# Mixer A's tiles first with the projections spread over them, mixer B's by blocks of tokens with the output projection beside them

## The chip, the cores and the metric

The kernel runs on one core of a Trainium2 chip. The metric is the device time of one execution in microseconds. The engines named here are PE (TensorE: matmuls and transposes; PEld is its weight load), DVE (VectorE), ACT (ScalarE), POOL (GpSimd) and SP (SyncE, which issues the DMAs). Each takes its instructions in the order of its own queue.

## What is computed

One step of a one-layer encoder over 1024 prompt rows and 32 sample rows, 1024 wide, all in float32: a SwiGLU layer, a sub-layer of two attention mixers, and a second SwiGLU layer. The change lies in the middle one.

```python
h = adaln_in(x, gains[2], sh2, sc2)
qa, ka, va, qb, kb, vb = jnp.split(h @ w_in, SPLITS, axis=-1)
# mixer A: 8 heads x 64; a row reads its own chunk of 64 and the 8 before, clipped relative bias
# mixer B: 8 query heads, 2 key/value heads; own chunk and the 2 before, bucketed bias, sinks
oa, ob, rows = mixers(qa, ka, va, qb, kb, vb)
o = jnp.concatenate([rmsnorm(oa, group_gains[:WIDTH_A]),
                     rmsnorm(ob, group_gains[WIDTH_A:])], axis=-1) @ w_out
x = x + g2[:, None] * rmsnorm(o, gains[3])
```

The newest key and value rows of both mixers are outputs too.

## The kernel before

The 1056 rows are kept in three blocks of 384, 384 and 288 columns (`TB`), features on the partitions. [...]

**Projections.** `qk_proj` (L670) makes one query or key unit, two heads wide: for each block 24 matmuls into the bank `pq`. `v_proj` (L653) makes a value unit, 256 columns wide: for each of nine tiles of rows 24 matmuls into `pv`. There are four query and four key units for A (`load_qa`, `load_ka`), two value units for A (`load_va`), four query units for B (`load_qb`), and one unit with the keys and values of B. Before the tiles start, a loop over the blocks (L1069) runs B's key/value unit, B's query unit 0 and A's value unit 0, each block as soon as its normalised input `h2` is there (`need`). That input comes from `between` (L496): the residual with its norm, then the next norm. In both norms the squares are folded on DVE and POOL, PE sums them over the partitions (`pss`), DVE takes nine small steps for the reciprocal root (`ry`), and PE broadcasts it (`pr`).

**Tiles.** An attention tile is a pair of heads `p` and 128 rows `i`. `TileB` (L780) has two matmul pairs for the scores (`Sb`), an addition of the bias and a maximum on DVE, exponentials on ACT, a scaling, transposes on PE (`ppb`), and the product with the values (`po`). `TileA` (L718) is the same with up to 640 keys (`S`, `pp`, `po`). `TileS` (L847) is the sample's tile of a pair (`Ss`, `pps`). The list `tiles` (L1094) has 72 of them: B's four pairs (36 tiles), A's pairs 0 and 1 (18), then A's pairs 2 and 3 interleaved (18). The loop at L1232 walks over the list. A tile's scores are issued two tiles ahead for B and one for A (`lead`).

**What goes beside the tiles.** `fill` issues pieces of the remaining projections at an even rate, in two stages (`STAGES`, by tile number): over tiles 0 to 34 the units of B's queries 1 to 3, A's values 1 and A's K and Q of pair 0, over 37 to 54 the K and Q of pairs 1 to 3. `group_norm(tb, g)` normalises a block of B's output (g = 1) or A's (g = 0). It needs all four pairs of that mixer in the block. `out_piece` makes one eighth of the output projection of a block (24 matmuls, bank `wo`). It needs both group norms of the block. Five pieces are issued within the tile loop (`OUTS`), 19 after it.

**The order.** The order in which the source issues work is only a priority: a scheduler at build time moves instructions within each engine's queue, and pools of buffers bound how far (eight slots in `wpool` for weights, keys, queries and values; five in `hpool`; two double banks for scores).

Of the kernel before, what the change touches and what calls it, by code (L numbers as in the profile page):

```python
# [21 lines left out]
DEC = 32  # L22
# [18 lines left out]
GN1 = 55  # L41
# [16 lines left out]
PRIME = 0  # L58
PFILL = 5
KEARLY = 1  # L60
# [6 lines left out]
STAGES = ((0, 34), (37, 54))  # L67
RATE = 1.0
OUTS = (0,) * 13 + (1,) * 5
LAG = 0.5  # L70
# [4 lines left out]
def encoder_step(ctx: ExitStack, tc, x_prompt, x_sample, cache_a_k, cache_a_v, cache_b_k, cache_b_v,  # L75
# [66 lines left out]
    jp = consts.tile([128, 128], I32, name="jp")  # L142
# [637 lines left out]
    class TileB:  # L780
# [14 lines left out]
        def qk(self, hh):  # L795
            if hh:
                return
            p, i, k0, nt = self.p, self.i, self.k0, self.nt
            c, L = p // 2, 128 * nt
            T = self.T  # L800
            bias = prep[("B", p)]["bias"]
            S = p2("Sb")
            for h in range(2):
                cols = slice(128 * k0, 128 * k0 + L)
                te.matmul(S[:, h, :L], T[:, h, :], KSB[:, c, cols], start=True, stop=False)
                te.matmul(S[:, h, :L], T[:, 2 + h, :], KSB[:, c, cols], start=False, stop=True)
            ve.tensor_tensor(S[:, :, :L], S[:, :, :L], bias[:, :, 256 - L:256], op=OP.add)
            nm = small.tile([128, 2], F32, name="nmb")
            ve.tensor_reduce(nm, S[:, :, :L], axis=AX.X, op=OP.max, negate=True)
# [29 lines left out]
        def av(self):  # L839
# [4 lines left out]
               lambda j, h, kn: kvb[:, k0 + j, 128 + 64 * c:192 + 64 * c],  # L844
               O[tb][:, 4 + p, 128 * cc:128 * cc + 128])

    class TileS:  # L847
# [53 lines left out]
        def av(self):  # L901
# [6 lines left out]
            else:  # L908
                c = p // 2

                def vsl(j, h, kn):
                    return (cbv if j == 0 else kvbs[:, 128:256])[:kn, 64 * c:64 * c + 64]
# [10 lines left out]
    def start_qb(p, w):  # L923
# [3 lines left out]
        qs = small.tile([128, DEC], F32, name="qbs", bufs=2)  # L927
# [40 lines left out]
    def flow_ka(p, w):  # L968
# [3 lines left out]
        piece = qk_proj(w, KQ[:, 0, :], KQs[:, 0, :], 1.0)  # L972
# [3 lines left out]
    def flow_qa(p, w):  # L976
        KQ, KQs = kqa[p]
        piece = qk_proj(w, KQ[:, 1, :], KQs[:, 1, :], 0.125)
        for tb in range(3):
            yield from piece(tb)  # L980
# [43 lines left out]
    wkv, wq0, wv0 = split_vcols(w_in, 2048), load_qb(0), load_va(0)  # L1024
    kvb = wpool.tile([128, 8, 256], F32, name="vt", tag="w")
    kvbs = small.tile([32, 256], F32, name="vs", bufs=3)
    kv_piece, q0_piece, v0_piece = v_proj(wkv, kvb, kvbs), start_qb(0, wq0), start_va(0, wv0)
# [17 lines left out]
    def keys_new(t0, n):  # L1045

        pk = KBANK("pk", (128, 4, 128))
        for j in range(n):
            te.transpose(pk[:, j, :], kvb[:, t0 + j, 0:128], ident)
        for c in range(2):  # L1050
            cols = slice(128 * t0, 128 * (t0 + n))
            pkc = pk[64 * c:64 * c + 64, 0:n].rearrange("p a b -> p (a b)")
            ae.activation(KSB[0:64, c, cols], pkc, AF.Copy)
            ve.tensor_tensor(KSB[64:128, c, cols], pkc, KSB[0:64, c, cols], op=OP.subtract)

    def keys_sample():
        pk = KBANK("pk")
        te.transpose(pk[:, :DEC], kvbs[:, 0:128], ident[:DEC, :DEC])
# [4 lines left out]
    def rows_b():  # L1063
        dma.dma_start(nbk_p[0, 0].rearrange("t h d -> t (h d)"), kvb[:, 7, 0:128])
        dma.dma_start(nbv_p[0, 0].rearrange("t h d -> t (h d)"), kvb[:, 7, 128:256])
        dma.dma_start(nbk_s[0, 0].rearrange("t h d -> t (h d)"), kvbs[:, 0:128])
        dma.dma_start(nbv_s[0, 0].rearrange("t h d -> t (h d)"), kvbs[:, 128:256])

    for tb in range(3):  # L1069
        need(("h2", tb))  # L1070
        if tb == 0:
            keys_cached()
        for x in token_tiles(tb):
            run(kv_piece(*x))
        if tb == 2:
            KSB = wpool.tile([128, 2, 1024], F32R, name="KSB", tag="w")
            if PRIME:
                primed.append(load_qb(1))
            keys = [lambda: keys_new(0, 4), lambda: keys_new(4, 4), keys_sample]
        if tb == 2 and KEARLY == 1:  # L1080
            keys.pop(0)()
        run(q0_piece(tb))
        for i, x in enumerate(token_tiles(tb)):
            run(v0_piece(*x))
            if tb == 2 and KEARLY:
                keys and keys.pop(0)()
    for k in keys:
        k()
    rows_va(0)
    rows_b()  # L1090
# [4 lines left out]
    for kind, p in [("B", p) for p in range(4)] + [("A", 0), ("A", 1)]:  # L1095
        opens[len(tiles)] = [(kind, p)]
        tiles.append(TileS(kind, p))
        tiles += [(TileB if kind == "B" else TileA)(p, i) for i in range(8)]
    for _, p, i in sorted((i + LAG * (p - 2) + (0 if i < 0 else 0), p, i) for p in (2, 3) for i in range(-1, 8)):
        if i < 0:  # L1100
            opens[len(tiles)] = [("A", p)]
        tiles.append(TileA(p, i) if i >= 0 else TileS("A", p))
    whole = [max(n for n, t in enumerate(tiles) if isinstance(t, TileA) and t.i // 3 == tb) for tb in range(3)]
# [22 lines left out]
    COST = {"B": 10.6, "V": 23.4, "K": 10.6, "A": 10.6}  # L1126
# [78 lines left out]
    def lead(t):  # L1205

        return LEAD_B if t < 36 else 1

    ready.add(("B", 0))
# [15 lines left out]
    with tc.manual_schedule(engines={mybir.EngineType.PE}) if MANUAL else ExitStack():  # L1225
# [3 lines left out]
        if PRIME == 2:  # L1229
            now = flow(flows[0][2])  # L1230
            fill(PFILL)
        for n in range(N):  # L1232
            for first, last, units in flows:
                if n == first:
                    now = now if PRIME == 2 and n == 0 else flow(units)
                    rate = sum(COST[key[0]] for key, _, _ in units) / (last - first) / 2 * RATE
# [6 lines left out]
            for _ in range(OUTS[n - 54] if n >= 54 else 0):  # L1243
# [14 lines left out]
            for _, last, _ in flows:  # L1258
                if n == last - 1:
                    fill(1e6)  # L1260
                    budget = 0.0
    tiles[N - 1].av()
    begin(("gn", 2, 0), group_norm(2, 0), first=True)
# [84 lines left out]
```

## Time and profile before

| | |
|---|---|
| three runs | 2225.36, 2229.99, 2230.26 us; median 2229.99 |
| profiled execution | 2232.07 us, its span 2230.3 us |
| granted TensorE clock, mean | 0.983 |
| mixer sub-layer within the span | 847 us (first `pv`) to 1429 us (last `wo`) |
| first score of B / of A | 933.0 us / 1084.9 us |

The span is the time from the first to the last instruction of the program, and the rest of an execution lies around it. In a row of a timeline the number in brackets is how long the engine stood idle before the instruction, and what ended that. In a row of groups the idle time stands behind the second bar. The rows of the profile stand in the prediction, where they are used.

### The profile page before, as it was taken

Reading aid. Unit: us, or ns where it says so; the run is one execution under the profiler, and the core shown is the slowest. Engines: PE = TensorE matmul, PEld = TensorE weight load, DVE = VectorE, ACT = ScalarE, POOL = GpSimd, SP = SyncE. Lnnn points to the kernel's source line nnn. Section 1 sums busy time; section 2 is a strip of 40 time slices with the busy share of each in tenths; the row PEclk is TensorE's granted clock in tenths of the full one; section 3 lists DMA queues with packets and bytes.
Section 4 is the critical chain, followed back from the end, with each engine's and each line's share of the span. In section 5 each row is a group of like instructions: output and inputs, shape, how many; then the busy total and the mean of one; then the engine's idle time right before and its main releaser. Section 6 shows DMA issues by size and latency. Waiting matters only on the chain.

```text
span 2230.3 us, 33962 instructions
## 1 busy us (share of the span) xinstructions
PE 2163.1 (97%) x14012; PEld 2069.8 (93%) x14012; DVE 1238.6 (56%) x2425; ACT 698.1 (31%) x1450; POOL 180.5 (8%) x281
## 2 busy tenths in 40 slices
PE   6989999999999999899999899999999999999998
PEld 4989999999999999899788579999999999999998
DVE  5735677765643497677544775775433333333336
ACT  4411111111111253566544763433111111111133
POOL 2100000000000022100110413320000000000000
PEclk8999999999999999899999899999999999999999
DMA  9245344343321353110211221523211111111122
GB/s 328 85 76 125 105 122 132 104 123 95 104 76 57 90 162 121 59 31 20 68 30 30 77 59 56 161 81 104 85 57 39 44 43 47 57 38 55 41 67 81
DMA packets 200350, 186.00 MB, mean 83 GB/s; under 512 B 7340, under 2 KB 169540, under 8 KB 199044
## 3 DMA queue, kind: packets, MB, share of 16 engines
q1 hardware_dynamic: 200196, 183.84, 27.7%
q8 instruction: 110, 1.80, 0.3%
q14 instruction: 44, 0.36, 0.1%
HBM read 160.98 MB, written 22.84 MB: 82 GB/s over the span
## 4 chain that ended last, share of the span: by engine, by line
PE 84%; DMA 7%; DVE 6%; ACT 1%; issue 1%; POOL 1%; SPq 0%; DVEq 0%; ACTq 0%; POOLq 0%
PE dn L316 7%; PE up L316 7%; PE up L318 7%; PE up L317 7%; PE dn L317 7%; PE dn L318 7%; PE gate L318 7%; PE gate L317 7%; PE gate L316 7%; DMA raw<-in_w_up_dram 4%; PE po L705 3%; PE S L744 2%; PE pq L316 2%; PE pq L318 2%; PE pq L317 2%; PE pp L768 1%
## 5 line engine op out<-in xcount | busy, mean ns | idle before, releaser
L316 PE MATMUL up<-h_hi,w 128*128 128x384 f32 (+1 forms) x1056 | 341.1, 323 | 9.2 <-ACT sl L541 9.2
L316 PE MATMUL dn<-gg,w 128*128 128x384 f32 (+1 forms) x1056 | 340.8, 324 | 3.9 <-DVE facc L572 3.5
L317 PE MATMUL gate<-h_lo,w 128*128 128x384 f32 (+1 forms) x1056 | 340.1, 322 | 3.9 <-DVE h_lo L437 3.9
L316 PE MATMUL gate<-h_hi,w 128*128 128x384 f32 (+1 forms) x1056 | 341.2, 323 | 0.0
L317 PE MATMUL up<-h_lo,w 128*128 128x384 f32 (+1 forms) x1056 | 340.8, 323 | 0.0
L317 PE MATMUL dn<-gg,w 128*128 128x384 f32 (+1 forms) x1056 | 339.8, 322 | 0.6 <-DVE gg L545 0.6
L318 PE MATMUL up<-h_hi,w 128*128 128x384 f32 (+1 forms) x1056 | 340.4, 322 | 0.0
L318 PE MATMUL gate<-h_hi,w 128*128 128x384 f32 (+1 forms) x1056 | 340.4, 322 | 0.0
L318 PE MATMUL dn<-gg,w 128*128 128x384 f32 (+1 forms) x1056 | 339.4, 321 | 0.0
L572 DVE TENSOR_TENSOR facc<-dn,facc 128x768 f32<-128x768 f32 (+1 forms) x240 | 212.7, 888 | 221.4 <-PE dn L318 221.3
L295 DVE TENSOR_TENSOR w<-raw,w 128x1024 fp32r<-128x1024 f32 x187 | 232.3, 1250 | 170.7 <-ACT w L294 163.6
L294 ACT ACTIVATE w<-raw 128x1024 fp32r<-128x1024 f32 x187 | 195.8, 1056 | 278.0 <-PE dn L318 103.5
L541 ACT ACTIVATE sl<-gate 128x384 f32<-128x384 f32 (+1 forms) x132 | 60.9, 462 | 549.6 <-PE gate L318 549.5
L542 DVE TENSOR_TENSOR sl<-sl,up 128x384 f32<-128x384 f32 (+1 forms) x132 | 68.5, 519 | 282.3 <-PE up L318 282.0
L316 PEld LDWEIGHTS up<-h_hi,w 128*128 128x128 f32 x1056 | 199.1, 189 | 9.5 <-ACT sl L541 9.5
L316 PEld LDWEIGHTS dn<-gg,w 128*128 128x128 f32 x1056 | 198.7, 189 | 5.8 <-DVE facc L572 4.8
L317 PEld LDWEIGHTS gate<-h_lo,w 128*128 128x128 f32 x1056 | 198.7, 188 | 4.5 <-DVE h_lo L437 4.5
L317 PEld LDWEIGHTS dn<-gg,w 128*128 128x128 f32 x1056 | 198.7, 188 | 1.2 <-DVE gg L545 1.2
L318 PEld LDWEIGHTS up<-h_hi,w 128*128 128x128 f32 x1056 | 199.4, 189 | 0.0
L317 PEld LDWEIGHTS up<-h_lo,w 128*128 128x128 f32 x1056 | 199.2, 189 | 0.0
L316 PEld LDWEIGHTS gate<-h_hi,w 128*128 128x128 f32 x1056 | 198.9, 188 | 0.1
L318 PEld LDWEIGHTS gate<-h_hi,w 128*128 128x128 f32 x1056 | 198.7, 188 | 0.0
(224 smaller groups left out, 3365.3 us busy)
## 6 DMA issues: line engine op xcount, KB each, us to landing
raw<-in_w_mod_dram SPq DMA_DIRECT2D x56, 512.0 KB, 4.0
raw<-in_w_gate_dram SPq DMA_DIRECT2D x54, 512.0 KB, 3.9
raw<-in_w_up_dram SPq DMA_DIRECT2D x54, 512.0 KB, 4.6
raw<-in_w_down_dram SPq DMA_DIRECT2D x54, 512.0 KB, 4.5
raw<-in_w_in_dram SPq DMA_DIRECT2D x18, 512.0 KB, 5.0
wm<-in_w_mod_dram SPq DMA_DIRECT2D x8, 1024.0 KB, 7.8
raw<-in_w_out_dram SPq DMA_DIRECT2D x13, 512.0 KB, 4.4
xr<-xs SPq DMA_DIRECT2D x16, 384.0 KB, 3.3
```

Of the source, the lines that this page charges most:

```text
L294: ae.activation(w[:, 0], r, AF.Copy)
L295: ve.tensor_sub(w[:, 1], r, w[:, 0])
L316: te.matmul(ps, w[:, 0, k], hi, start=start, stop=False)
L317: te.matmul(ps, w[:, 0, k], lo, start=False, stop=False)
L318: te.matmul(ps, w[:, 1, k], hi, start=False, stop=stop)
L541: ae.activation(sl[:, :w], ps[0][:, :w], AF.Silu)
L542: ve.tensor_tensor(sl[:, :w], sl[:, :w], ps[1][:, :w], op=OP.mult)
L572: ve.tensor_tensor(o, ps[:, :, :w], o, op=OP.add)
L705: te.matmul(po[64 * h:64 * h + 64, :n], vsl(j, h, kn), PT(h, j, kn), start=j == 0, stop=j == nt - 1)
L744: te.matmul(S[:, c:ce], self.T[:, h, :], KQ[:, 0, 128 * k0 + c:128 * k0 + ce], start=True, stop=True)
L768: te.transpose(pp[:, j - j0, :], P[:, 128 * j:128 * j + 128], ident)
```

## The change

Mixer A's tiles come first, pair by pair. Before them the opening loop runs A's key unit 0, value unit 0 and query unit 0. One flow of units is spread over tiles 0 to 42 at an even rate: K1, Q1, V1, K2, Q2, K3, Q3, then B's keys and values, then B's four query units. B's 36 tiles follow, by block of rows: for block 0 each pair's sample tile and tiles 0 to 2, for block 1 tiles 3 to 5 of each pair, for block 2 tiles 6 and 7. A's group norms are started at tile 44, and B's for a block two tiles after its last tile (tiles 51 and 63; block 2 after the loop). Twelve output pieces go beside tiles 57 to 71. B's four biases take one buffer of `wpool` instead of one each of `rpool`.

```diff
-GN1 = 55
+GN1 = 44
...
-STAGES = ((0, 34), (37, 54))
+UNITS = 42
 RATE = 1.0
-OUTS = (0,) * 13 + (1,) * 5
-LAG = 0.5
+OUTS = {n: 1 for n in (57, 58, 59, 60, 61, 62, 64, 66, 68, 69, 70, 71)}
...
     def prepare(kind, p):
         if kind == "B":
-            bias = rpool.tile([128, 2, 256], F32, name="bias", tag="r")
+            if p == 0:
+                prep["bias_b"] = wpool.tile([128, 4, 2, 256], F32, name="bias_b", tag="w")
+            bias = prep["bias_b"][:, p]
...
-    wkv, wq0, wv0 = split_vcols(w_in, 2048), load_qb(0), load_va(0)
+    wk0, wv0, wq0 = load_ka(0), load_va(0), load_qa(0)
+    k0_piece, v0_piece, q0_piece = start_ka(0, wk0), start_va(0, wv0), start_qa(0, wq0)
+    B = {}
...
+    def flow_kvb(_, ws):
+        B["kv"] = wpool.tile([128, 8, 256], F32, name="vt", tag="w")
+        B["kvs"] = small.tile([32, 256], F32, name="vs", bufs=3)
+        piece = v_proj(ws, B["kv"], B["kvs"])
+        keys_cached()
+        for tb in range(3):
+            for x in token_tiles(tb):
+                yield from piece(*x)
+            if tb == 1:
+                B["K"] = wpool.tile([128, 2, 1024], F32R, name="KSB", tag="w")
+                keys_new(0, 4)
+        keys_new(4, 4)
+        keys_sample()
+        rows_b()
...
     for tb in range(3):
         need(("h2", tb))
-        if tb == 0:
-            keys_cached()
+        run(k0_piece(tb))
         for x in token_tiles(tb):
-            run(kv_piece(*x))
+            run(v0_piece(*x))
         if tb == 2:
...
+            primed.append(load_ka(1))
         run(q0_piece(tb))
...
-    for kind, p in [("B", p) for p in range(4)] + [("A", 0), ("A", 1)]:
...
+    for p in range(4):
+        opens[len(tiles)] = [("A", p)]
+        tiles.append(TileS("A", p))
+        tiles += [TileA(p, i) for i in range(8)]
+    for tb in range(3):
+        for p in range(4):
+            if tb == 0:
+                opens[len(tiles)] = [("B", p)]
+                tiles.append(TileS("B", p))
+            tiles += [TileB(p, i) for i in range(8) if i // 3 == tb]
...
-    flows = [(*STAGES[0], unit_qb(1) + unit_qb(2) + unit_qb(3) + unit_va(1) + unit_qka(0)),
-             (*STAGES[1], unit_qka(1) + unit_qka(2) + unit_qka(3))]
...
+    units = unit_qka(1) + unit_va(1) + unit_qka(2) + unit_qka(3) + unit_kvb()
+    for p in range(4):
+        units += unit_qb(p)
...
-        return LEAD_B if t < 36 else 1
+        return 1 if t < 36 else LEAD_B
...
             if n == GN1:
                 for tb in range(3):
-                    begin(("gn", tb, 1), group_norm(tb, 1))
+                    begin(("gn", tb, 0), group_norm(tb, 0))
             for tb in range(2):
                 if n == whole[tb] + 2:
-                    begin(("gn", tb, 0), group_norm(tb, 0), first=True)
+                    begin(("gn", tb, 1), group_norm(tb, 1), first=True)
```

What the scheduler makes of it is shown at three places of PE's queue. The line numbers of the changed kernel differ by three in most places.

First, the opening: block 2's second norm, with its sums `pss` and its broadcast `pr`. Before, value matmuls (`pv`) of block 1 stand ahead of the sums:

```order
L662 MATMUL pv<-w,h_hi 128x256
L663 MATMUL pv<-w,h_lo 128x256
L348 MATMUL pss<-ones,sq 128x1 x2
L348 MATMUL pss<-ones,sq 32x1
L348 MATMUL pss<-ones,sq 128x1 x2
L348 MATMUL pss<-ones,sq 32x1
L396 MATMUL pr<-ident,ry 128x128 x2
L396 MATMUL pr<-ident,ry 128x32
L661 MATMUL pv<-w,h_hi 128x256
```

Now:

```order
L313 MATMUL pq<-h_hi,w 128x384
L314 MATMUL pq<-h_lo,w 128x384
L315 MATMUL pq<-h_hi,w 128x384
L345 MATMUL pss<-ones,sq 128x1 x2
L345 MATMUL pss<-ones,sq 32x1
L345 MATMUL pss<-ones,sq 128x1 x2
L345 MATMUL pss<-ones,sq 32x1
L393 MATMUL pr<-ident,ry 128x128 x2
L393 MATMUL pr<-ident,ry 128x32
L313 MATMUL pq<-h_hi,w 128x288
```

Between the residual's `pr` and these sums there stood 7 query and 72 value matmuls, and now there stand 24 query matmuls.

Second, a pair of B tiles in block 0 or 1, with the transposes of the probabilities (`ppb`) and the products with the values (`po`). Before, pieces of a query unit (`pq`) stand between them:

```order
L834 MATMUL ppb<-ident,Pb 128x128 x2
L316 MATMUL pq<-h_hi,w 128x288
L317 MATMUL pq<-h_lo,w 128x288
L318 MATMUL pq<-h_hi,w 128x288
L316 MATMUL pq<-h_hi,w 128x288
L317 MATMUL pq<-h_lo,w 128x288
L318 MATMUL pq<-h_hi,w 128x288
L705 MATMUL po<-PTb,vt 64x128 x2
L834 MATMUL ppb<-ident,Pb 128x128 x2
L705 MATMUL po<-PTb,vt 64x128 x2
```

Now, for the tiles after the last projection:

```order
L831 MATMUL ppb<-ident,Pb 128x128 x4
L702 MATMUL po<-PTb,vt 64x128 x4
L393 MATMUL pr<-ident,ry 128x128 x3
L831 MATMUL ppb<-ident,Pb 128x128 x4
L802 MATMUL Sb<-KSB,qs 128x256
L803 MATMUL Sb<-KSB,qs 128x256
L802 MATMUL Sb<-KSB,qs 128x256
L803 MATMUL Sb<-KSB,qs 128x256
L702 MATMUL po<-PTb,vt 64x128 x4
```

From the last `pq` to the first `wo` the queue holds the scores of 14 B tiles, two sample tiles and the norms' sums and broadcasts, and nothing else.

Third, tiles of A in pairs 2 and 3 with 640 keys (scores `S` in two pieces, transposes `pp`). Before:

```order
L768 MATMUL pp<-ident,P 128x128 x4
L705 MATMUL po<-PT,vt 64x128
L744 MATMUL S<-KQ,qz 128x512
L744 MATMUL S<-KQ,qz 128x128
L768 MATMUL pp<-ident,P 128x128 x5
L705 MATMUL po<-PT,vt 64x128 x8
```

Now:

```order
L765 MATMUL pp<-ident,P 128x128 x4
L313 MATMUL pq<-h_hi,w 128x384
L314 MATMUL pq<-h_lo,w 128x384
L315 MATMUL pq<-h_hi,w 128x384
L313 MATMUL pq<-h_hi,w 128x384
L314 MATMUL pq<-h_lo,w 128x384
L315 MATMUL pq<-h_hi,w 128x384
L741 MATMUL S<-KQ,qz 128x512
L741 MATMUL S<-KQ,qz 128x128
L765 MATMUL pp<-ident,P 128x128 x4
```

Projection pieces stand between A's tiles now, but not everywhere: 84 query matmuls stand in one lump ahead of pair 2's last needs, and five or so tiles behind it have none.

More of the change, by code (lines that the diff above doesn't have):

```diff
@@ L139, in encoder_step @@
         XIN[0] = load_x(0)
-    jp = consts.tile([128, 128], I32, name="jp")
+    jp = s_tile([128, 128], "jp", I32)
     ge.iota(jp, pattern=[[1, 128]], base=0, channel_multiplier=-1)
@@ L926, in start_qb @@
         qt = qb["t"][:, p % 2, :]
-        qs = small.tile([128, DEC], F32, name="qbs", bufs=2)
+        qs = small.tile([128, DEC], F32, name="qbs", bufs=4)
         qb[p] = (qt, qs)
@@ L971, in flow_ka, with start_qa @@
         kqa[p] = (KQ, KQs)
-        piece = qk_proj(w, KQ[:, 0, :], KQs[:, 0, :], 1.0)
+        return qk_proj(w, KQ[:, 0, :], KQs[:, 0, :], 1.0)
+    def start_qa(p, w):
+        KQ, KQs = kqa[p]
+        return qk_proj(w, KQ[:, 1, :], KQs[:, 1, :], 0.125)
+    def flow_ka(p, w):
+        piece = start_ka(p, w)
         for tb in range(3):
@@ L976, in flow_qa @@
     def flow_qa(p, w):
-        KQ, KQs = kqa[p]
-        piece = qk_proj(w, KQ[:, 1, :], KQs[:, 1, :], 0.125)
+        piece = start_qa(p, w)
         for tb in range(3):
@@ L1099, in encoder_step @@
[L1099 to L1103, printed above, removed]
+    for p in range(4):
+        opens[len(tiles)] = [("A", p)]
+        tiles.append(TileS("A", p))
+        tiles += [TileA(p, i) for i in range(8)]
@@ L1104, in encoder_step @@
+    for tb in range(3):
[4 more added lines that the diff above has]
+            tiles += [TileB(p, i) for i in range(8) if i // 3 == tb]
+    whole = [max(n for n, t in enumerate(tiles) if isinstance(t, TileB) and t.i // 3 == tb) for tb in range(3)]
     ready = set()
@@ L1228, in encoder_step @@
         scores(-1, 1)
-        if PRIME == 2:
-            now = flow(flows[0][2])
-            fill(PFILL)
+        now = flow(units)
+        rate = sum(COST[key[0]] for key, _, _ in units) / UNITS / 2 * RATE
         for n in range(N):
[L1233 to L1236, printed above, removed]
             if n == GN1:
                 for tb in range(3):
-                    begin(("gn", tb, 1), group_norm(tb, 1))
+                    begin(("gn", tb, 0), group_norm(tb, 0))
             for tb in range(2):
                 if n == whole[tb] + 2:
-                    begin(("gn", tb, 0), group_norm(tb, 0), first=True)
-            for _ in range(OUTS[n - 54] if n >= 54 else 0):
+                    begin(("gn", tb, 1), group_norm(tb, 1), first=True)
+            for _ in range(OUTS.get(n, 0)):
                 if outs and n >= whole[outs[0][0]] + 2:
@@ L1257, in encoder_step @@
                 fill(rate)
[L1258 to L1261, printed above, removed]
+            if n == UNITS:
+                fill(1e6)
+                now = None
     tiles[N - 1].av()
-    begin(("gn", 2, 0), group_norm(2, 0), first=True)
+    begin(("gn", 2, 1), group_norm(2, 1), first=True)
     while outs:
```

57 lines of the change are left out of this document (20 added, 37 removed).

## The prediction

> **What bounds the kernel now.** I read the page first, then busy time by stage, then the waits of PE inside the mixer sub-layer. The page:
>
> ```profile
> span 2230.3 us, 33962 instructions
> PE 2163.1 (97%) x14012; PEld 2069.8 (93%) x14012; DVE 1238.6 (56%) x2425; ACT 698.1 (31%) x1450; POOL 180.5 (8%) x281
> PE   6989999999999999899999899999999999999998
> PEclk8999999999999999899999899999999999999999
> ```
>
> PE is the bound, and the FFN slices cannot improve: all 9s. The dents lie in the mixer sub-layer, from the first projection to the last output projection (847 to 1429 us). I cut it where the instruction names change: the projections that open it; mixer B's 36 tiles with projections between them; mixer A's first 18 tiles with the rest of the projections; its last 18 tiles, alone until 1297, then with output pieces; the remaining output pieces. The columns are the stretch and its length, then the busy time (and count) of PE, PEld, DVE, ACT and POOL, the granted clock, and DMA.
>
> ```profile
> 847.00:933.00 86.00, 80.53 (x615) 78.57 (x614) 58.16 (x145) 35.85 (x81) 21.49 (x23) 0.94 0.23 77
> 933.00:1087.00 154.00, 148.56 (x1150) 133.10 (x1151) 111.73 (x396) 104.99 (x363) 12.46 (x44) 0.97 0.14 39
> 1087.00:1232.00 145.00, 142.74 (x963) 116.77 (x962) 67.14 (x165) 65.81 (x170) 17.75 (x62) 1.00 0.13 36
> 1232.00:1297.00 65.00, 59.08 (x384) 38.54 (x385) 53.13 (x157) 46.37 (x115) 25.04 (x59) 0.89 0.19 54
> 1297.00:1344.00 47.00, 46.34 (x330) 39.12 (x330) 31.54 (x71) 32.18 (x60) 7.79 (x10) 1.00 0.32 91
> 1344.00:1429.00 85.00, 81.80 (x526) 80.74 (x526) 55.89 (x113) 36.28 (x61) 29.44 (x20) 0.98 0.27 90
> ```
>
> See three things. The fourth stretch, A tiles with nothing beside them, has the lowest clock, 0.89, and PE idles 6 us. In the second, where B runs beside projections, DVE (112 of 154 us) and ACT (105) are nearly as loaded as PE; in the third, A beside projections, they are half empty (67 and 66 of 145). The first is disturbed at one place.
>
> **Prices on PE.** A matmul in a dense stream costs the distance to the next start:
>
> ```profile
> 890.65 0.34 PE L316 MATMUL pq<-h_hi,w 128*128 128x384 f32 x1
> 890.82 0.34 PE L317 MATMUL pq<-h_lo,w 128*128 128x384 f32 x1
> 892.04 0.28 PE L661 MATMUL pv<-w,h_hi 128*128 128x256 f32 x1
> 892.16 0.28 PE L662 MATMUL pv<-w,h_hi 128*128 128x256 f32 x1
> ```
>
> So 0.174 us for 384 columns, 0.12 for 256, and, scaled by width, 0.131 for 288. A query or key unit (48 matmuls of 384 columns, 24 of 288, from the code) is 11.5 us; a value unit (216 of 256) is 25.9. Take these out of the dense stretches: the second holds five query/key units and one value unit, 83.4 us, which leaves 71 us for 36 B tiles, **2.0 us a B tile**. The third holds six units, 69 us, which leaves 76 us for 18 A tiles, **4.2 us an A tile**. Both include the cost of switching between kinds of matmul. No arithmetic is added or removed; PE's instruction counts stay. So the change can only move waits.
>
> **Gain 1: the bare A tiles get cover.** The last 18 A tiles took 65 + 47 = 112 us. Of that the output pieces are
>
> ```profile
> 1297.00:1344.00 47.00, 23.50 (x126) 21.38 (x126) 2.46 (x5) 1.00 0.32 91
> ```
>
> (the matmuls of `wo` alone) 126 at 0.174, 22 us. The other 90 us did 18 A tiles, where the dense price is 76. With projections beside them: **-14 us**. The group norms' few matmuls that were in the 90 reappear in the B stretch below, whose price includes them.
>
> **Gain 2: the hand-over from B to A.** PE's waits in the sub-layer show it stopping there for the first A bank and its cache rows:
>
> ```profile
> PE S L744 <- ACT Ps L880: 1.3, 1, 1.3
> PE po L705 <- ACT o L697: 2.3, 3, 1.3
> PE pkc L1019 <- DMA ck<-in_cache_a_k_dram: 1.2, 1, 1.2
> ```
>
> The three longest, 1.3 + 1.3 + 1.2 = 3.8 us, lie between 1079 and 1089 us. In the new order the hand-over (A to B) has query pieces queued around it, and B's biases are all in one tile prepared ahead: **-4 us**. The first sample tile after the opening stays uncovered as now, only that it is A's: nothing.
>
> **Cost 1: less cover for the third block's normalised input.** Before PE can project block 2, its residual and norm chain must end. These are PE and DVE at that place:
>
> ```profile
> 889.50 0.94 PE L396 MATMUL pr<-ident,ry 128*128 128x128 f32 x6
> 890.48 4.49 DVE L455 SCALAR_TENSOR_TENSOR facc<-facc,gcoef,pr 128x256 f32<-128x256 f32 x16 [5.68 <-PE pr L396]
> 900.05 0.46 DVE L361 TENSOR_TENSOR sq<-sq 128x288 f32<-128x288 f32 x1
> 904.10 1.01 PE L396 MATMUL pr<-ident,ry 128*128 128x128 f32 x6 [2.44 <-DVE ry L329]
> 906.23 0.58 PE L661 MATMUL pv<-w,h_hi 128*128 128x256 f32 x1 [1.11 <-ACT h_hi L435]
> 907.00:914.00 7.00, 4.35 (x21) 3.75 (x20) 0.00 (x0) 0.50 0.00 0
> ```
>
> From the broadcast `pr` at 889.5 to the folded squares at 900.5 the chain takes 11 us, and PE has 72 value matmuls and 7 query ones to fill it, 9.9 us. The opening now runs K0, V0 and Q0 (11.5 + 25.9 + 11.5) instead of kvB, qB0 and vA0 (25.9 + 11.5 + 25.9): 14 us of work leave for the fill later, which is neutral, but between those two rows only 24 query matmuls stand, 4.2 us (first pair of order pieces), and 24 + 43 + 87 matmuls in the whole chain from block 1's broadcast, 22.3 us where it was 28.8. So PE waits 6.5 us more, and behind the waiting `pr` stand in its queue block 2's whole share of K0, V0 and Q0 and, behind those, all of A. The waits of 2.4 and 1.1 us stay, and the half clock that follows them (0.50 in the last row, 21 matmuls in 7 us) starts from a longer gap, which I put at 2 us more. **+9 us**; bounds 0 (if the chain, with less beside it on DVE and ACT, comes earlier by as much) and +11.
>
> **Cost 2: B tiles without cover.** The projections end with query unit 3, all by tile 42. The first output piece needs both halves of block 0's group norm, and B's half of it exists only when tile 51 is done. In the program's order PE then does the scores of 14 B tiles, two of them with a sample tile, with no projection and no output piece beside them (second pair of pieces). Their dense PE price is 28 us. What DVE does for them in that stretch, by its rows in the second stretch:
>
> ```profile
> L807 DVE TENSOR_TENSOR Sb<-Sb,bias 128x512 f32<-128x512 f32 (+1 forms) x32 | 21.1, 663 | 14.9 <-PE Sb L806 14.4
> L809 DVE TENSOR_REDUCE nmb<-Sb 128x2 f32<-128x512 f32 (+1 forms) x32 | 21.0, 655 | 0.7
> L716 DVE TENSOR_TENSOR qs<-qbt,qs 64x128 fp32r<-64x128 f32 x58 | 16.4, 282 | 1.2
> L295 DVE TENSOR_TENSOR w<-raw,w 128x1024 fp32r<-128x1024 f32 x3 | 3.7, 1219 | 1.9 <-ACT w L294 1.9
> L311 DVE TENSOR_TENSOR w<-raw,w 128x1024 fp32r<-128x1024 f32 x2 | 2.5, 1225 | 0.4 <-ACT w L310 0.4
> ```
>
> DVE is busy 111.7 us there; less the weight splits (3.7 + 2.5) that is 105.5 over 36 tiles, 2.9 us a tile, 42 us for 14.5. ACT by the same division is 2.7. The three group norms of A and the first of B fall into the same stretch. From 1232 to 1344, where four started, DVE spent on them:
>
> ```profile
> L1142 DVE SCALAR_TENSOR_TENSOR z<-o,cst,rstd 128x384 f32<-128x384 f32 x12 | 8.3, 739 | 0.5 <-ACT rstd L1137 0.5
> L1147 DVE TENSOR_TENSOR o_lo<-z,o_hi 128x768 fp32r<-128x768 f32 x3 | 3.9, 1309 | 2.1 <-ACT o_hi L1146 2.1
> L328 DVE SCALAR_TENSOR_TENSOR rt<-rt,rv 128x3 f32<-128x3 f32 x12 | 2.0, 164 | 0.2
> ```
>
> 8.3 + 3.9 and three times 2.0 for the rsqrt steps, 18.2 for three finished, and one weight split is 1.2: DVE needs 42 + 18 + 1 = **61 us** before the output pieces can run in full, and PE has 28 us of work. **+33 us.** Bounds: 0, if DVE gets ahead during the A stage, where it is half empty; +61, if PE and DVE alternate instead of overlapping (28 + 61). I take DVE's sum, to which the order binds it. Behind each PE wait there stand only the next B tile's scores and transposes, and DVE and ACT wait for those in turn; the output pieces come last.
>
> **Cost 3: a bare patch inside A.** The scores of pair 2 may not open before its K and Q units are done, so the order runs 84 query matmuls in one lump, and about five A tiles behind it stand bare. Bare A tiles cost 90/76 of dense ones: 5 x 4.2 x 0.18 = **+4 us** (bounds 0 and +8).
>
> The moved loads cost nothing:
>
> ```profile
> raw<-in_w_in_dram SPq DMA_DIRECT2D x18, 512.0 KB, 5.0
> ```
>
> Each is issued one unit ahead, 11.5 us of work or more, and takes 5.0 us to land. They are as many as before, and SP's queue has no instruction that PE waits for in between, apart from the new biases of B, all into one buffer. That buffer and B's keys share the eight slots with K/Q, V and weights; if a slot comes late a unit starts later, which cost 3's upper bound takes in. Without that cover a load would show as 5 us a unit.
>
> After the bare stretch come ten B tiles beside 12 output pieces: PE 20 + 12 x 4.2 = 70 us and more, DVE 10 x 2.9 + two norms + splits, under 60: dense. The closing chain of block 2's norm keeps its 2.4 us wait. The second FFN starts from the same state.
>
> **Sum:** -14 - 4 + 9 + 33 + 4 = **+28 us** on a profiled execution of 2232.07 us (span 2230.3): 2260. The median of the runs shown is 2 us lower, so I predict **2258 us**.
>
> **Rivals.**
> *Faster: DVE is ahead.* A's stage leaves DVE 78 of 145 us free. If the group norms of pairs 0 to 2 and the splits ran there, and two tiles of lookahead kept PE fed, costs 1 to 3 vanish and the gains stay: -18, **2212**. It decides as soon as the bare stretch lasts under 46 us, given costs 1 and 3 vanish too. Against: a score needs its matmul first, at most two tiles ahead, and the norms begin at tile 44. Chance 0.13.
> *No change.* The norms' 18 us hide in B's own gaps and the stretch lasts 42 us (+14), cost 1 stays hidden: -18 + 14 + 4 = 0, **2230**. Chance 0.12.
> *Much slower: half clock.* If the bare stretch drops the clock as at 907 us, PE's 28 us become 56, no longer beside DVE's 61 but in turn with it, since each tile goes PE, DVE, ACT, PE, DVE, PE. Half of it exposed is +28 more: **2286**. Chance 0.13.
>
> [...]
>
> **How the numbers follow.** Forecast 0.62, its own range 2240 to 2275. To leave no more than two in ten outside, the range reaches half into both outer rivals: **2215 to 2285**. A measurement of this kernel tells about 0.3% (7 us) from no change. Faster takes the first rival, 0.13; same the second, 0.12; slower the rest, 0.75.
>
> **What would show it.** Right: after 1180 us or so, a stretch of some 60 us between the last query projection and the densest output pieces with DVE busy over 50 of 60 and PEld under half; PE waiting before block 2's first projection 6 us longer; DVE's rows for p = 2, 3 of A spread with PEld near 0.8. Wrong: PE busy over 90% with clock 1.00 all through the B stage, or an A stage that costs more than 4.2 us a tile beside its projections.

## The result, and the profile after

The changed kernel takes 2276.9 us (median of four runs, 2275.2 to 2278.57) beside 2228.5 us of the kernel before in the same session: **2.2% slower**, ratio 1.0219 with a 95% interval of 1.0201 to 1.0236. The profiled execution has a span of 2276.8 us, 46.5 more than before. The prediction said 2258 us, slower, in a range of 2215 to 2285: the direction held, and 19 us of the loss were not in its sum.

The page of the changed kernel:

```profile
span 2276.8 us, 33944 instructions
PE 2175.8 (96%) x14012; PEld 2084.3 (92%) x14012; DVE 1240.9 (55%) x2425; ACT 699.7 (31%) x1450; POOL 175.3 (8%) x281
PE   6989999999999998999999797999999999999998
PEclk9999999999999998999999789999999999999999
```

As many matmuls as before. The dents now lie together: in the 23rd slice (each is 57 us) a 7 stands in PE's row and in the clock's, and in the 25th another in PE's.

Busy time by stage, cut where the names change: the opening; A's tiles in two parts; the last query units beside the first B tiles; B tiles with nothing; four stretches of B tiles with output pieces; the last pieces. Columns as in the prediction.

```profile
847.00:926.00 79.00, 67.30 (x471) 65.24 (x472) 48.34 (x124) 28.11 (x64) 22.05 (x31) 0.89 0.21 72
926.00:1087.00 161.00, 155.85 (x1106) 128.19 (x1102) 72.60 (x180) 76.57 (x187) 19.26 (x76) 0.97 0.18 52
1087.00:1215.00 128.00, 128.00 (x907) 106.76 (x907) 61.63 (x158) 61.80 (x161) 9.75 (x42) 0.98 0.11 29
1215.00:1258.00 43.00, 42.52 (x318) 38.68 (x318) 25.80 (x88) 23.80 (x80) 1.85 (x6) 1.00 0.22 62
1258.00:1324.00 66.00, 45.46 (x269) 35.48 (x270) 59.66 (x212) 45.51 (x153) 16.54 (x24) 0.64 0.03 9
1324.00:1372.00 48.00, 48.00 (x330) 44.98 (x330) 43.79 (x119) 36.75 (x97) 9.74 (x15) 1.00 0.23 67
1372.00:1392.00 20.00, 15.24 (x100) 13.41 (x100) 17.30 (x60) 14.42 (x46) 6.27 (x7) 0.83 0.01 1
1392.00:1416.00 24.00, 23.23 (x155) 21.50 (x153) 11.07 (x29) 11.82 (x23) 3.04 (x3) 1.00 0.29 83
1416.00:1434.00 18.00, 7.17 (x32) 6.40 (x32) 10.04 (x27) 3.58 (x6) 2.87 (x3) 0.62 0.26 95
1434.00:1474.00 40.00, 40.00 (x288) 40.00 (x287) 30.27 (x51) 22.01 (x36) 17.53 (x11) 1.00 0.40 136
```

See three dark rows. 1258 to 1324 is the bare B stretch, 66 us with DVE busy for 59.7 of it. 1372 to 1392 is a dip among the tiles that have output pieces. 1416 to 1434 is the closing chain of block 2's norm, in which PE works 7 of 18 us. The first was in the prediction. The second was not, and the third only as a wait of 2.4 us.

PE's waits, first in the opening (847 to 926), then from 1416 on:

```profile
PE pss L345 <- POOL sq L358: 4.8, 1, 4.8
PE pv L660 <- DVE h_lo L434: 2.5, 1, 2.5
PE pr L393 <- DVE ry L326: 2.4, 1, 2.4
PE pq L313 <- ACT h_hi L432: 1.3, 1, 1.3
...
PE po L702 <- DVE fo L452: 4.5, 1, 4.5
PE pss L345 <- POOL sq L358: 4.1, 1, 4.1
PE pr L393 <- DVE ry L326: 2.3, 1, 2.3
```

The 4.8 us are the uncovered normalised input of block 2. The last three, 10.9 us, follow one another. In the kernel before, the same place (1344 to 1429) has these waits:

```profile
PE pr L396 <- DVE ry L329: 2.4, 1, 2.4
PE pss L348 <- POOL sq L361: 0.8, 2, 0.6
```

In the changed kernel the last tile's product waits for a bank that DVE's residual of block 0 is still reading, then the sums wait for the squares of block 2 behind it, then the broadcast waits for the root.

Where DVE's 59.7 us of the bare stretch go (group rows: line, operation, count, busy us, mean ns, idle before):

```profile
L712 DVE CAST qs<-qbt 64x128 fp32r<-64x128 f32 x26 | 11.2, 432 | 0.5
L804 DVE TENSOR_TENSOR Sb<-Sb,bias_b 128x512 f32<-128x512 f32 (+1 forms) x14 | 9.2, 656 | 1.1 <-PE Sb L803 1.0
L806 DVE TENSOR_REDUCE nmb<-Sb 128x2 f32<-128x512 f32 (+1 forms) x14 | 9.0, 644 | 0.1
L713 DVE TENSOR_TENSOR qs<-qbt,qs 64x128 fp32r<-64x128 f32 x26 | 7.4, 283 | 0.7
L1157 DVE SCALAR_TENSOR_TENSOR z<-o,cst,rstd 128x384 f32<-128x384 f32 x7 | 4.1, 614 | 0.1
L324 DVE TENSOR_TENSOR rt<-ry 128x3 f32<-128x3 f32 x9 | 1.4, 161 | 0.2
L1162 DVE TENSOR_TENSOR o_lo<-z,o_hi 128x768 fp32r<-128x768 f32 x1 | 1.0, 959 | 0.0
```

Group norms take 10.3 us of it: 4.1 + 1.0, three kinds of root steps at 1.4 (one is shown) and two rows of 0.5. One weight split takes 1.2 (weights and activations are kept as a high and a low part, and a product is three matmuls), and the tiles have the other 48. The longest of PE's waits in the stretch are for ACT and for DVE:

```profile
PE Sb L802 <- ACT Pb L813: 4.5, 4, 2.7
PE po L702 <- ACT PTb L694: 4.4, 4, 2.1
PE po L702 <- DVE PTb L692: 3.5, 1, 3.5
PE Sb L802 <- DVE qs L712: 2.7, 1, 2.7
```

### The profile page after: what moved, and what is told of

Same layout as the page of the kernel before. It is cut to its first block, busy times and chain, and to the rows that moved or that the text cites. A ratio compares the mean times of both kernels' runs of the same rounds, so it can differ in the third digit from the quotient of the medians.

```text
span 2276.8 us, 33944 instructions
## 1 busy us (share of the span) xinstructions
PE 2175.8 (96%) x14012; PEld 2084.3 (92%) x14012; DVE 1240.9 (55%) x2425; ACT 699.7 (31%) x1450; POOL 175.3 (8%) x281
## 5 line engine op out<-in xcount | busy, mean ns | idle before, releaser
L313 PEld LDWEIGHTS dn<-gg,w 128*128 128x128 f32 x1056 | 199.6, 189 | 4.6 <-DVE facc L569 4.1
L314 PEld LDWEIGHTS dn<-gg,w 128*128 128x128 f32 x1056 | 199.9, 189 | 1.0 <-DVE gg L542 0.9
L313 PEld LDWEIGHTS gate<-h_hi,w 128*128 128x128 f32 x1056 | 198.8, 188 | 1.6 <-ACT h_hi L432 1.5
L315 PEld LDWEIGHTS dn<-gg,w 128*128 128x128 f32 x1056 | 199.7, 189 | 0.0
```

What stands on the lines that cost most here:

```text
L313: te.matmul(ps, w[:, 0, k], hi, start=start, stop=False)
L314: te.matmul(ps, w[:, 0, k], lo, start=False, stop=False)
L315: te.matmul(ps, w[:, 1, k], hi, start=False, stop=stop)
```

## The experiments

"Bare stretch" is from the last query matmul to the first output matmul (65.9 us in the changed kernel, counted exactly). "Lost" is the length of a stretch less PE's matmuls in it at their distance in a dense stream, as in the prediction, and less 0.1 us for each switch from one kind of matmul to another. The 0.1 us is an estimate from the dense stretches of both traces, where it leaves less than 2 us over. Stretches are compared within the sub-layer, because the part ahead of it varies: the trace of experiment 1 reaches the first projection at 842.8 us and that of the changed kernel at 847.0, though the edit lies far behind it.

**1. The closing wait.** The three last pieces of block 1, 72 matmuls, stand in PE's queue behind block 2's norm. Here they go ahead of it.

```diff
     tiles[N - 1].av()
+    for _ in range(3):
+        out_piece()
     begin(("gn", 2, 1), group_norm(2, 1), first=True)
```

> The changed kernel (2276.9 us) with its three last output pieces of block 1 written before the start of block 2's group norm. In the changed kernel they stand on PE's queue behind that norm's sums and broadcast, and PE waits 4.5 + 4.1 + 2.3 us there (10.9 us) between 1416 and 1431 us. Theory 'place in the queue': the 72 matmuls (12.5 us) fill the wait, at most the 2.3 us wait for ry stays: 2267 to 2269 us. Rival 'the chain itself is late': the norm's chain starts later by as much as the pieces take and the wait moves behind them: 2274 to 2278 us.

Measured: 2283.6 us, ratio 1.0243 (1.0227 to 1.0258), slower than the change itself and above both ranges. The trace agrees with the first theory up to the end of the sub-layer: from the first projection to the last output matmul it takes 618.9 us, where it was 626.5, 7.6 less. But the 803.3 us from there to the end became 817.7. In the second FFN's opening, 1462 to 1540 us, PE now waits 15.4 us in all:

```profile
PE pss L345 <- POOL sq L358: 7.8, 1, 7.8
PE gate L314 <- DVE h_lo L434: 3.4, 2, 2.8
PE pr L393 <- DVE ry L326: 2.8, 1, 2.8
PE gate L313 <- ACT h_hi L432: 1.4, 1, 1.4
```

In the changed kernel there were 4.7:

```profile
PE gate L314 <- DVE h_lo L434: 3.3, 1, 3.3
PE gate L313 <- ACT h_hi L432: 1.4, 1, 1.4
```

The 24 pieces also cover the residuals and norms of three blocks, which lead into the second FFN. Pieces spent early on one of these chains are missing beside the next. The second theory had the right idea and too near a place.

**2. More cover in the bare stretch.**

```diff
-UNITS = 42
+UNITS = 46
```

> The changed kernel with the projections spread over 46 tiles instead of 42. In the order the last query matmul moves behind the scores of 9 B tiles instead of 6, and 11 B tiles instead of 14 stand bare before the first output piece. Theory 'DVE's sum, PE without cover' (66 us for 14 tiles against 27 us of PE's work, 2.8 us lost a tile): three tiles get cover, 2267 to 2271 us, bare stretch near 52 us. Rival 'the same loss elsewhere' (the A stage has less beside it, or DVE sets the pace beside the query pieces too): 2274 to 2279 us.

Measured: 2282.4 us, ratio 1.0235 (1.0218 to 1.0252). The last B score to be covered moved as expected (11 tiles have their scores in the bare stretch), but the bare stretch still takes 58.6 us for 11 tiles, 5.3 a tile where it was 4.7. The part ahead of it, B tiles beside query pieces, was dense in the changed kernel (lost 1.8 of 40.6 us) and now loses 12.1:

```profile
1209.00:1271.00 62.00, 55.55 (x399) 49.30 (x399) 35.10 (x135) 32.87 (x115) 5.73 (x12) 0.94 0.10 28
1271.00:1329.40 58.40, 35.63 (x211) 28.31 (x209) 51.15 (x167) 40.14 (x126) 15.64 (x22) 0.64 0.03 10
```

DVE is busy for 35 of 62 us in the first row, so DVE's load is not what holds it. PE waits there 6.5 us in all for ACT, 2.5 of them at once, with query pieces queued behind the wait. The time lies above even the rival's 2274 to 2279 us: the loss was not only moved, it grew.

**3 and 4. Less DVE work in the bare stretch, by moving it.** First the cast of the query to POOL, then mixer A's norms earlier.

```diff
-SPLIT = "vav"
+SPLIT = "gav"
```

> The changed kernel with one of the three steps that split a B tile's query (the CAST on DVE, 26 times 0.43 us = 11.2 us in the bare stretch) on POOL instead, which is busy 17 of 66 us there. Theory 'DVE's sum': the bare stretch shrinks from 66 to 55 to 58 us and the dip at 1372 to 1392 us by some, 2262 to 2269 us. Rival 'latency' (each tile goes PE, DVE, ACT, DVE, PE in turn, DVE's load is incidental): a copy on POOL takes longer than on DVE, 2276 to 2285 us.

```diff
-GN1 = 44
+GN1 = 38
```

> The changed kernel with mixer A's group norms started at tile 38 instead of 44. In the order two group norms instead of three have their sums in the bare stretch. Theory 'DVE's sum': the norms' rows on DVE in the bare stretch (z 4.1, the small steps and o_lo 6.2, 10.3 us for three) fall by a third or more and the stretch by 3 to 6 us, 2271 to 2274 us. Rival 'latency': a norm lies beside the tiles' own waits, 2276 to 2278 us.

Measured: 2277.9 us (1.0217, 1.0201 to 1.0232) and 2279.8 us (1.0226, 1.0211 to 1.0241). The bare stretches shrank to 63.6 and 63.5 us with DVE busy 55.0 and 56.4. The part ahead, from the first B score to the last query matmul, grew from 40.6 to 45.8 and 48.9 us, with 6.8 and 6.9 lost there. In both, what the stretch gave was spent before it began. The first time is the rival's, which here can't be told from the change, and the second lies 2 us above its rival.

The first edit takes 11.2 us of casts off DVE, but only 4.5 us of DVE's busy time go. POOL needs 0.33 us for each cast, and DVE's 26 subtractions at L713 took 11.3 us instead of 7.4. Alone each took 0.26 to 0.29 us, and beside an instruction of POOL up to 1.80. So the load was in part exchanged and not cut, and this run is a weak test of "DVE's sum".

**5. Less DVE work, by leaving it out.**

```diff
-            ve.tensor_tensor(S[:, :, :L], S[:, :, :L], bias[:, :, 256 - L:256], op=OP.add)
```

> The changed kernel (2276.9 us) without the addition of the bias to B's prompt scores on DVE, which is left out of the computation: 14 times 0.66 = 9.2 us of DVE's 59.7 busy us in the bare stretch of 66 us, and nothing else moves to another engine. Theory 'DVE's sum': the stretch falls to 57 to 59 us and the dip at 1372 to 1392 us by a few, 2262 to 2268 us. Rival 'in turn' (PE at half clock, DVE, ACT and PE again, two tiles in flight): half of it shows, 2271 to 2274 us. Rival 'given back elsewhere' (as three cuts before this one were): 2275 to 2282 us.

Measured: 2270.2 us, ratio 1.0184 (1.0169 to 1.0199): 6.7 us less than the change, just under the range of "in turn" and above that of "DVE's sum". The bare stretch is 62.2 us with DVE at 53.4, so 6.1 us less of DVE gave 3.7 us. The 9.2 us of the additions did not all come off: other instructions of DVE took longer, the subtractions at L713 for one 8.2 us instead of 7.4.

**6. The clock in the bare stretch.** Eight more matmuls behind each bare tile's scores, into unused columns of the same bank.

```diff
+            if (i // 3 == 0 and p >= 2) or (i // 3 == 1 and 3 * p + i - 3 < 8):
+                for j in range(8):
+                    te.matmul(S[:, j % 2, 256:512], T[:, j % 2, :], B["K"][:, c, 0:256], start=True, stop=True)
```

> The changed kernel with eight more matmuls of 256 columns behind the scores of each of the 14 bare B tiles, into columns of the score bank that nothing reads (13.4 us of PE's work at full clock, in a stretch of 66 us in which PE had 27 us of work, was busy 45 us and had a clock of 0.64). Theory 'half clock decides': the clock rises to 0.9 or more, the scores, transposes and products of a tile take half as long, the stretch falls to 55 to 60 us, 2266 to 2271 us. Theory 'DVE's sum': the clock rises and the stretch stays, 2275 to 2279 us; if DVE has to wait for the added matmuls as well, up to 2290 us.

Measured: 2274.6 us, ratio 1.0209 (1.0191 to 1.0227), which cannot be told from the change and lies 0.4 us under the second theory's range. The stretch:

```profile
1254.00:1320.00 66.00, 54.02 (x385) 45.26 (x384) 57.27 (x212) 46.11 (x156) 17.19 (x24) 0.84 0.03 9
```

The clock rose from 0.64 to 0.84, short of the 0.9 that the theory asked for, and the stretch took 65.7 us as before. PE did 13 us of matmuls more in the same time. So the half clock alone does not set the length of the stretch. That it costs nothing is not shown: the added matmuls stand in PE's queue behind the scores, and DVE's additions waited 3.4 us for them, where they waited 1.0 us for the scores in the change.

**7. A third tile in flight.**

```diff
-LEAD_B = 2
+LEAD_B = 3
...
-            S = p2("Sb")
+            if n_b[0] % 2 == 0:
+                n_b.append(p2("Sb", (128, 2, 2, 256)))
+            S = n_b[-1][:, n_b[0] % 2]
+            n_b[0] += 1
```

> The changed kernel with the scores of B issued three tiles ahead instead of two, two tiles sharing one double bank. Theory 'DVE's sum': DVE is busy 59.7 of 66 us in the bare stretch, so at most its 6 us of gaps go, 2271 to 2277 us. Rival 'too few tiles in flight': the waits go in the bare stretch and in the dip at 1372 to 1392 us (7 us) alike, 2262 to 2268 us.

Measured: 2289.2 us, ratio 1.0271 (1.0256 to 1.0287). Both theories missed. The bare stretch takes 67.7 us, and the tiles beside output pieces 105.1 where they took 97.6. Why a third tile makes it longer is not shown.

**8. The first gain alone, in the kernel before.**

```diff
-STAGES = ((0, 34), (37, 54))
+STAGES = ((0, 34), (37, 60))
...
-LAG = 0.5
+LAG = 8
```

> The kernel before (2229 us) with mixer A's last two pairs one after the other instead of interleaved, and the second stage of projections spread over tiles 37 to 60 instead of 37 to 54: nine bare A tiles instead of 18, and 4 output pieces beside tiles instead of 5. It does the change's first gain alone. Theory 'bare A tiles cost 0.75 us each or more' (17 us lost in 18 of them): 2220 to 2224 us. Rival 'the cover is only moved' (the first 18 A tiles have less of it, block 0's pieces come later): 2227 to 2233 us.

Measured: 2233.2 us beside 2229.9, ratio 1.0018 (1.0009 to 1.0027): the rival. Here is the stretch from the last projection to the first output piece, in this kernel (first row), and in the kernel before:

```profile
1232.00:1308.00 76.00, 64.41 (x394) 42.39 (x394) 61.68 (x168) 51.11 (x116) 25.54 (x49) 0.85 0.23 64
```

```profile
1220.00:1297.00 77.00, 70.53 (x473) 46.15 (x473) 60.32 (x172) 52.79 (x133) 27.95 (x72) 0.91 0.21 60
```

With a longer spread there are fewer scores in it (75 matmuls of `S` instead of 80), and it is as long, with 23.7 us lost instead of 17.3. The edit did not bring the nine bare tiles that were expected: of the 192 score matmuls of A, 84 still come after the last projection, where 104 did. So this run does not show what cover for all bare A tiles is worth. In both kernels, and in the changed one, the time between the last projection and the first output piece is the longest in which PE starves. This spread does not shorten it.

**9. Output pieces spread evenly.**

```diff
-OUTS = {n: 1 for n in (57, 58, 59, 60, 61, 62, 64, 66, 68, 69, 70, 71)}
+OUTS = {n: 1 for n in (57, 59, 61, 63, 65, 67, 69, 71)}
```

> The changed kernel (2276.9 us) with eight output pieces in the tile loop, one beside every second tile from 57 to 71, instead of twelve (six in a row, then gaps). In the changed kernel PE loses 12.7 us between the first piece and the last B product (7 of them at 1372 to 1392 us, where block 0's pieces are used up and block 1's norm is not done) and 8.5 us from there to the last piece. Theory 'the places of the pieces': the dip goes, the closing chain has eight more pieces ahead of it, 2262 to 2269 us. Rival 'DVE paces these tiles whatever PE has': the B tiles with half a piece each stretch by as much, 2274 to 2284 us.

Measured: 2270.9 us, ratio 1.0182 (1.0165 to 1.0199), 6.0 less than the change. The gain did not come where it was looked for. From the first piece to the last product 16.6 us are lost (12.7 in the change), since tiles that have half a piece each wait for ACT. Behind that the waits, 1322 to 1474 us:

```profile
PE ppb L831 <- ACT Pb L819: 6.5, 4, 2.5
PE pss L345 <- POOL sq L358: 4.1, 3, 2.7
PE pr L393 <- DVE ry L326: 2.3, 1, 2.3
```

The 4.5 us wait of the last product is gone. So are 4.7 of the 5.3 us lost in the 60 us after the last piece. From the first projection to the last output matmul the trace takes 626.0 us, where it was 626.5: what this edit gained lies behind the sub-layer.

**10. Cover for block 2's input.** Key unit 1 moves from the flow into the opening loop.

```diff
-    wk0, wv0, wq0 = load_ka(0), load_va(0), load_qa(0)
+    wk0, wv0, wq0, wk1 = load_ka(0), load_va(0), load_qa(0), load_ka(1)
...
+    k1_piece = start_ka(1, wk1)
...
         run(q0_piece(tb))
+        run(k1_piece(tb))
...
-    units = unit_qka(1) + unit_va(1) + unit_qka(2) + unit_qka(3) + unit_kvb()
+    units = unit_qka(1)[1:] + unit_va(1) + unit_qka(2) + unit_qka(3) + unit_kvb()
...
```

> The changed kernel with A's key unit 1 taken out of the flow beside the tiles and run in the opening loop, behind Q0 of each block: 8.4 us of matmuls more between the broadcasts of blocks 1 and 2. The opening loses 12.6 us (before: 5.5 to 6.1), 4.8 of them in one wait for the folded squares of block 2. Theory 'cover for block 2's input' (cost 1): the loss of the opening falls to 6 to 8 us and the A tiles stay dense, 2270 to 2273 us. Rival 'the cover is only moved': 2275 to 2279 us.

Measured: 2272.1 us, ratio 1.0193 (1.0178 to 1.0208), the first theory's number. The 4.8 us wait for the folded squares is gone from the opening, which loses 7.4 us where it lost 12.6:

```profile
PE pv L660 <- DVE h_lo L434: 2.5, 1, 2.5
PE pr L393 <- DVE ry L326: 2.4, 1, 2.4
PE pq L313 <- ACT h_hi L432: 1.3, 1, 1.3
```

The A tiles, with 11.5 us less beside them, lose no more than they did (7.7 us, 11.7 in the change). But the B stage lost 8.5 us more in this trace, 2.4 in the bare stretch and 6.1 from there to the last product. From the first projection to the last output matmul the trace takes 625.7 us, only 0.8 less than the change. So the wait is mended, but that the time of the kernel fell by this is not shown: of the trace's shorter span 4.2 us lie before the first projection, where traces of unlike edits differ as much (842.8 in experiment 1).

**11. No sums for A's norms.**

```diff
-        pr = yield from mean_rstd(O[tb], range(4 * g, 4 * g + 4), w, 2.0 / D, JG, p1)
...
-        ae.activation(r[:, :w], pr[:, :w], AF.Copy)
+        if g:
+            pr = yield from mean_rstd(O[tb], range(4 * g, 4 * g + 4), w, 2.0 / D, JG, p1)
+            ae.activation(r[:, :w], pr[:, :w], AF.Copy)
+        else:
+            ae.activation(r[:, :w], O[tb][:, 0, :w], AF.Copy)
```

> The changed kernel with the squares, sums, reciprocal root and broadcast of mixer A's three group norms left out of the computation (a copy takes the place of the broadcast); the scaling and the splitting stay. Two of the three stood in the bare stretch (66 us, DVE 59.7). Theory 'load of DVE': 20 small steps, 3.3 us, of which 0.6 shows as in the cuts before, the stretch falls by 2 us, 2274 to 2276 us. Rival 'the sums on PE's queue': PE stops for the squares folded on POOL (2.3 us) and for the root, with scores behind them, and the tiles start late each time, the stretch falls by 6 us or more, 2268 to 2272 us.

Measured: 2274.3 us, ratio 1.0203 (1.0187 to 1.0218), the first theory's number, though it cannot be told from the change either. The stretch is 63.3 us, a little less than that theory had. It fell by 2.6 us, where the rival asked for 6 or more, so the sums on PE's queue are not most of what starts the tiles late. The first theory's mechanism is not shown: DVE is busy for 58.9 us, only 0.6 less, because more of the norms' scaling now falls into the stretch (12 rows of `z` with 6.5 us instead of 7 with 4.1).

**12. Both gains together** (the edits of 9 and 10).

> The changed kernel (2276.9 us) with both edits that gained alone: key unit 1 in the opening loop (-4.8 us alone) and eight output pieces, one beside every second tile (-6.0 us alone). Theory 'two separate losses' (the opening's wait and the end of the B stage): the gains add, 2264 to 2268 us, still above the kernel before (2229 us) by what the bare B stretch costs. Rival 'one pace' (what comes earlier is lost again in the B stage, whose loss rose by 8.5 us when the opening alone was mended): 2269 to 2273 us.

Measured: 2269.8 us, ratio 1.0181 (1.0165 to 1.0197): the second theory. The opening keeps its gain and the B stage gives most of it back, as in 10. No arrangement tried here beat the kernel before.

## Why the prediction was right in direction and short in size

- **Gains 1 and 2 and cost 3 came as forecast in their sum.** From the first sample score (926) to the last query matmul (1258) are 332 us. At the prediction's prices, 36 A tiles (151), six key and query units (69), value unit 1 and B's keys and values (51.8), four query units of B (46) and six B tiles (12) make 330. So the A tiles were dense as a whole, and the patch inside A and the hand-over came to 2 us together, where cost 3 less gain 2 had 0. PE waits 4.2 us in this stretch for the sample's exponentials, of which 3.3 are the first sample tile behind the opening, a wait that the kernel before had as 2.4 in front of `Sb`. At the hand-over to B it has no wait over 0.5 us (1087 to 1258). One reading behind the price of 4.2 us was off: the last query matmul of the kernel before starts at 1219.7 us, so 12 us of the "dense" third stretch had no projections.
- **Cost 1 held.** The opening took 79 us. Before it took 86, with 14.4 us more of units. That is +7.4 us for a forecast of 9 within 0 and 11. The new wait is 4.8 us, not 6.5, and stood at the predicted place. Experiment 10 removed it with cover alone, so the mechanism of the wait is shown.
- **Cost 2: the size was near, the reason only in part.** 66 us for 61, a loss of 38 for 33. DVE's load was 59.7 for 61, but by two errors that cancel: the tiles took 48 us, not 42, and the norms 10, not 18. Of the tiles' 6 us more, 5 are casts that took longer beside POOL (last section). Of the norms' 8 us less, 4 are scalings (7 in the stretch, not 12) and 3 are splits (one on DVE, not three). That the stretch is DVE's sum is too much said. Cuts of 4.5, 3.2 and 6.1 us of DVE gave 2.3, 2.4 and 3.7 us, between a half and three quarters, while in experiment 11 0.6 us less of DVE went with 2.6. Between 4 and 9 us beside DVE's busy time stay in every version. That the order on three engines in turn takes the rest is the likeliest reading of PE's waits on ACT and DVE, but no run shows it, and which link of it was not settled.
- **The rival "half clock" fell in its mechanism.** The clock did drop, to 0.64, but the stretch took 5 us more than forecast, where the rival added 28, and with the clock raised to 0.84 it was as long (experiment 6). That the time lies nearer to this rival's 2286 us than to 2258 is chance: what was missing lay behind the stretch.
- **The step that failed** is the sentence after the moved loads: "After the bare stretch come ten B tiles beside 12 output pieces [...] dense. The closing chain of block 2's norm keeps its 2.4 us wait." The order leaves twelve tiles' scores and 16 tiles' products behind the first piece, not ten tiles. From the first to the last output matmul the changed kernel takes 149.9 us and loses 21.2. The kernel before takes 131.7 and loses 5.7. That is **+15 us** at a forecast of nothing, nearly the whole miss. The waits show where: 10.9 us in the closing chain (3.2 before), and 5 in the dip at 1372 to 1392, with the low clock of 0.83 and 0.62 around them. The prediction spent twelve pieces beside tiles and did not ask what the closing chains would be covered by. In the kernel before, 451 output matmuls (19 pieces) come after the last tile's product, and now 264 do (11 pieces). Experiment 1 shows that the loss is shared between these chains. Moving pieces ahead of one took 7.6 us from it and put 14.4 into the next.
- "The second FFN starts from the same state" missed by 1.5 us (803.3 for 801.8).

The parts, -14 + 2 + 7.4 + 38 + 15 + 1.5, add to 50 where the spans differ by 46.5, since each price is a mean over a stretch. Counted as lost time in both kernels the sum closes better: 6.5 to 7 us in the opening (12.6 for 5.5 to 6.1), about 1 up to the last query matmul, 21 from there to the first output matmul (38 for 17.3), 15.5 to the last one and 1.5 behind, 45 to 46. In this count gain 1 and cost 2 together are the 21, where the forecast had -14 + 33. Two things stay open: why work taken out of the bare stretch was lost again beside the query pieces ahead of it (experiments 2 to 4), and what a third tile in flight ran into.

## What to carry to other kernels

Count what each piece of independent work covers, not only whether it can be moved: here the same 24 output pieces cover the last tiles, a group norm and three residual chains, and whoever takes a piece from one owes it to the next. Ask which tiles lose most without cover: here a bare B tile lost 2.7 us (38 for 14, with three group norms among them) and a bare A tile 0.8 (14 for 18). When a price rests on the sum of one engine's work, a cut in that work is the test: in three such cuts half to three quarters came back in its own stretch, and in two of these it was lost again ahead of it. Look in the trace at how much of the cut really left the engine.

## What the runs showed of the hardware

The granted TensorE clock fell from 1.00 to 0.53 after waits of at most 0.8 us. These windows of the changed kernel begin the bare stretch:

```profile
1260.00:1262.00 2.00, 1.41 (x14) 1.00 (x15) 1.94 (x6) 1.94 (x7) 0.00 (x0) 1.00 0.00 0
1262.00:1264.00 2.00, 1.12 (x12) 0.67 (x11) 1.91 (x8) 1.33 (x7) 0.00 (x0) 1.00 0.28 77
1264.00:1266.00 2.00, 1.07 (x6) 0.69 (x6) 1.97 (x10) 1.11 (x7) 0.00 (x0) 1.00 0.62 185
1266.00:1270.00 4.00, 2.15 (x18) 1.45 (x18) 3.69 (x15) 4.00 (x18) 2.29 (x4) 0.53 0.00 0
```

Up to 1266 the longest single wait was 0.8 us, with PE busy for 1.1 to 1.4 of every 2 us, and in the 4 us behind that the clock was 0.53.

A cast on DVE took 1.83 us beside an instruction of POOL, and 0.22 us as the median of 64. In the first of these views are POOL's rows of the changed kernel from 1281 us, in the second DVE's:

```profile
1283.00 1.83 POOL L1162 TENSOR_TENSOR o_lo<-z,o_hi 128x768 fp32r<-128x768 f32 x1 [1.62 <-ACT o L694]
```

```profile
1283.09 2.19 DVE L712 CAST qs<-qbt 64x128 fp32r<-64x128 f32 x2
```

The two casts took 2.19 us. The first alone took 1.83 us: POOL began 0.09 us ahead of it, and it ended 0.1 us after POOL's instruction did. Behind them the next scores waited 2.7 us on PE. The same happened again at 1307 us, where one cast took 1.73. In the whole bare stretch the 26 casts took 11.2 us, and at the mean of the kernel before (0.227 us) they would have taken 5.9. Nine of them took over 0.3 us, each with an instruction of POOL beside it. The kernel before never showed a cast over 0.65 us: its casts ran between 910 and 1070 us, and its POOL splits at L1147 from 1255 us on.
